# Stick-breaking scores of two heads in two 64-row halves of the PE array, with one transposition bank instead of two

## The chip, the cores and the metric

The kernel runs on one core of one Trainium2 chip. The metric is the device time of one execution in microseconds (us). PE is TensorE, the matrix engine; DVE, ACT and POOL are VectorE, ScalarE and GpSimd; SP issues DMAs.

## The reference

One layer: RMSNorm, one input projection, eight stick-breaking heads and four differential heads, a gate, one output projection with the residual, a final RMSNorm. 1024 tokens and 16 meta tokens, width 1024, all float32. The part that the change touches is the scores z and the weights w made of them:

```python
for t0 in range(0, Lp, Q_BLOCK):                       # Q_BLOCK = 128, head width d = 64
    z = einsum('bqhd,bkhd->bhqk', q[:, t0:t1], k[:, :t1]) * d ** -0.5
    strict = arange(t1)[None, :] < arange(t0, t1)[:, None]
    log_beta = log_sigmoid(z)
    log_keep = where(strict, log_sigmoid(-z), 0.0)
    stick = pad(cumsum(log_keep[..., 1:], axis=3, reverse=True), ...)
    w = where(strict, exp(log_beta + stick), 0.0)
    o = einsum('bhqk,bkhd->bqhd', w, v[:, :t1])
```

## The kernel before

Tokens run in reverse order, so that the stick-breaking product is a forward scan. The work is cut into eight groups: groups 0 to 3 hold two stick-breaking heads each, groups 4 to 7 one differential head each. A float32 product is made of float32r passes over an exact hi + lo split of both operands.

While a group's attention runs, the four projections of the next group (q, v, k, gate: `mm3`, L154 to L156, three passes per k-tile) are woven into it: `weave` takes from either generator by a ratio of planned times. A scheduler then sets the final order on each engine, and gives tiles the buffers that are free at that place of its plan. Each engine works through its own list in that order. So PE finds projection products between the steps of the attention, and where the list has none, it stands until the step before has come through the other engines.

One stick-breaking group goes over 8 query blocks of 128 rows; block b sees 1040 - 128 b keys. In what follows b0 is the widest (1040 columns, in chunks of 348, 346, 346), b1 has 912 (2 x 456), b2 784, b3 656, b4 528, b5 400, b6 272, b7 144. A step for one head and one block (a head-block):

- `qk` (L461, L462): scores. q is stacked as [hi; lo] in 128 rows, k hi and k lo are each there twice, so two passes of 128 rows carry the three products. Tiles z, three PSUM banks.
- `sb_weights`: the mask on the first 128 columns (DVE, L473), two sigmoids per chunk (ACT, L474 to `keep`, L475 to `beta`), the scan over `keep` (DVE, L478), its product with `beta` (DVE, L480), a small copy (POOL, L481). `beta` and `keep` come from a pool of four buffers with the tag be.
- `sb_transpose`: 128 x 128 transpositions of beta (PE, L499) in batches of up to four into a bank tr, each batch copied to wt by ACT (L500). Two tr banks.
- `sb_pv` (L521): weights times v for two blocks; the two heads stand in two 64-column halves of the array.

The heads take turns: transposition of head 0's last block, scores and weights of head 0, the same for head 1. `stack_q` and `stack_k` make the doubled operands with moves by DMA on SP's queue: nine in a stick-breaking group. Groups 4 to 7 use the same `qk` with their own stacking, and the same z and tr banks (transpositions at L624 and L658, copies at L625).

Of the kernel before, what the change touches and what calls it, by code (L numbers as in the profile page):

```python
"""Hybrid trunk layer: stick-breaking heads and differential heads side by side.

Tokens run in reverse order on the chip (r = 1039 - position): the stick-breaking
product is then a forward scan, and a query block sees a suffix of the keys.
float32 products run as three float32r passes over an exact hi + lo split of both
operands; where a head is only 64 deep, q is stacked [hi; lo] so that two passes
over the duplicated k hi and k lo carry the whole product.
"""
# [17 lines left out]
P = 128  # L26
D = 1024
SEQ = 1024
# [24 lines left out]
class Build:  # L53
# [15 lines left out]
    # ---------------------------------------------------------------- pools  # L69
    def open(self):  # L70
# [4 lines left out]
            for t, n in (("mm", 2), ("z", 3), ("tr", 2), ("pv", 1))  # L75
# [12 lines left out]
    # ------------------------------------------------------------ constants  # L88
# [21 lines left out]
    def df_constants(self):  # L110
# [8 lines left out]
        # -lambda on every partition  # L119
# [16 lines left out]
    # ----------------------------------------------------------- projection  # L136
    def w_half(self, u, h, copy=None, room=None):
        """load half of a 128-column unit of w_in and split it into hi + lo"""
# [8 lines left out]
    def mm3(self, ps, w, kt, c0, cn):  # L147
        """one k-tile of a projection, three passes"""
# [18 lines left out]
    def proj_last(self, u, chs, post):  # L167
        """the last projection goes k-tile by k-tile, and w_out takes the place of x behind it"""
# [30 lines left out]
    def evac_rope(self, t):  # L199
        """t = x * cos + swap(x) * sin, with rstd in both tables"""  # L200
# [14 lines left out]
    def stack_q(self, t, st, sb):  # L215
        """[hi; lo] for the first 64-deep half, [hi; lo] for the second, scale folded in"""
# [3 lines left out]
        lo = self.tl(self.tp, [P, T], F32R, "t")[:, :SEQ]  # L220
# [3 lines left out]
        if sb:  # L224
            self.move(b[0:64], a[64:128])
            self.move(b[64:128], lo[64:128])
            self.move(a[64:128], lo[0:64])
        else:
            for r in (0, 64):
                self.move(b[r + 32:r + 64], a[r + 32:r + 64])  # L230
                self.move(b[r:r + 32], lo[r + 32:r + 64])
                self.move(a[r + 32:r + 64], lo[r:r + 32])
        st["q"] = (a, b)

    def stack_k(self, t, st, sb):
        """[hi; hi] and [lo; lo] for both halves"""
        nc = self.nc
        ha, hb, la, lb = (self.tl(self.a2, [P, T], F32R, n) for n in ("ha", "hb", "la", "lb"))
        nc.scalar.copy(out=ha, in_=t)
        nc.vector.tensor_sub(la, t, ha.bitcast(F32))  # L240
        for a, b in ((ha, hb), (la, lb)):
            for r, n in ((0, 64),) if sb else ((0, 32), (64, 32)):
# [5 lines left out]
    def make_v(self, t, st, sb, on_pe):  # L248
        """token-major v tiles: by transposition on PE where they are needed soon, else by
        32x32 transposition on DVE, the blocks put in place by DMA"""  # L250
# [26 lines left out]
    def make_vr(self, st, sb):  # L277
        """the rows of v that the tiles leave out"""
# [16 lines left out]
    def make_gate(self, g, sb):  # L295
        """g * sigmoid(g); among exponentials the sigmoid waits for the whole width, to
        change the function table once"""
# [28 lines left out]
    def project(self, gi, st, first=False):  # L326
        """generator: the four projections of a group and what attention needs of them"""
# [34 lines left out]
    def start(self, st):  # L362
        """x arrives k-tile by k-tile: split it, collect its squares, and run q, k, g of group 0"""
        nc, i = self.nc, self.i
        uq, uk, uv, ug = self.units(0)
        # the array clock rises under load: bring it up while the first tiles travel
# [10 lines left out]
        plan = [(uq, CH_Q, "mm"), (uk, CH_K, "z"), (ug, CH_Q, "tr")]  # L377
        banks = [[self.bank(tag) for _ in chs] for _, chs, tag in plan]
# [86 lines left out]
    def sb_weights(self, st, hd, b):  # L465
# [4 lines left out]
        for c0, cn in chunks(kw):  # L470
            z = self.qk(st, hd, b, c0, cn)
            if c0 == 0:
                nc.vector.tensor_add(z[:, :P], z[:, :P], self.zmask)  # L473
# [451 lines left out]
```

## Time and profile before

| what | value |
|---|---|
| median of 3 runs | 703.42 us (702.63 to 705.86) |
| profiled execution, from its first to its last instruction | 703.8 us |
| PE busy | 683.9 us (97%) |
| DVE busy | 510.6 us (73%) |
| ACT busy | 367.2 us (52%) |

The profiled execution has no time of its own besides its span, which lies 0.4 us above the median of the runs. Busy time of PE is the union of its products as they are drawn; a product is drawn longer than the distance to the next one, since products overlap in the array. What one of them costs is therefore read from the distance between starts, not from its length.

### The profile page before, as it was taken

The page shows a single profiled execution, that of the slowest core. Times are in us where ns is not written, and L with a number is a line of the kernel's source. Part 1 is how long each engine was busy: PE and PEld are TensorE (multiplying, and loading weights), DVE is VectorE, ACT ScalarE, POOL GpSimd, SP SyncE. Part 2 cuts the span into 40 slices and gives each one's busy share as a digit, 9 for nine tenths or more (in the row PEclk, how much of TensorE's full clock was granted, in tenths as well). Part 3 has the DMA queues.
Part 4 walks back from the last instruction along what each step waited for, and adds up shares of the span by engine and source line. Part 5 has one row for each costly group of instructions (what it writes and reads, how often), then busy time and mean ns, then how long its engine had stood idle before and what let it go on. Part 6 is the DMA issues. An engine that isn't in the chain of part 4 may idle for free.

```text
span 703.8 us, 11492 instructions
## 1 busy us (share of the span) xinstructions
PE 683.9 (97%) x4016; PEld 590.8 (84%) x4016; DVE 510.6 (73%) x1028; ACT 367.2 (52%) x961; POOL 150.0 (21%) x195
## 2 busy tenths in 40 slices
PE   8899999999999999989999999999999999999996
PEld 6699988788978897778878998899889987888885
DVE  6945887589667975697856877787678688777653
ACT  6512655555545554655543656555655545665542
POOL 4711011212011211131220112211212053011222
PEclk9999999999999999999999999999999999999998
DMA  8317224122341225122351225132503663221322
GB/s 306 121 46 167 75 48 113 53 62 65 76 100 61 61 57 126 38 60 61 61 136 60 62 60 136 32 93 59 137 30 90 157 235 128 64 83 61 117 86 94
DMA packets 59049, 64.67 MB, mean 92 GB/s; under 512 B 31088, under 2 KB 39408, under 8 KB 58992
## 3 DMA queue, kind: packets, MB, share of 16 engines
q1 hardware_dynamic: 58848, 63.94, 32.8%
q8 instruction: 32, 0.52, 0.3%
q14 instruction: 25, 0.20, 0.1%
q10 hardware_dynamic: 144, 0.00, 0.0%
HBM read 34.37 MB, written 7.34 MB: 59 GB/s over the span
## 4 chain that ended last, share of the span: by engine, by line
PE 82%; DVE 10%; issue 2%; DMA 2%; ACT 2%; POOL 1%; SPq 0%; POOLq 0%; DVEq 0%; ACTq 0%
PE mm L154 15%; PE mm L155 15%; PE mm L156 14%; PE mm L703 10%; PE pv L521 6%; PE tr L499 4%; PE z L461 4%; PE z L462 4%; PE pv L641 4%; PE tr L624 2%; DVE be L478 1%; DVE nm L580 1%; DVE xl L393 1%; DVE wt L144 1%; DMA t<-xT 1%
## 5 line engine op out<-in xcount | busy, mean ns | idle before, releaser
L154 PE MATMUL mm<-xh,wh 128*128 128x346 f32 (+2 forms) x592 | 211.8, 359 | 2.5 <-DVE be L208 2.0
L155 PE MATMUL mm<-xl,wh 128*128 128x346 f32 (+2 forms) x592 | 210.8, 356 | 0.4 <-DVE xl L393 0.3
L156 PE MATMUL mm<-xh,wl 128*128 128x346 f32 (+2 forms) x592 | 211.0, 357 | 0.0
L154 PEld LDWEIGHTS mm<-xh,wh 128*128 128x128 f32 x592 | 112.4, 190 | 13.0 <-DVE be L208 2.7
L156 PEld LDWEIGHTS mm<-xh,wl 128*128 128x128 f32 x592 | 112.3, 190 | 10.7 <-issue 1.7
L155 PEld LDWEIGHTS mm<-xl,wh 128*128 128x128 f32 x592 | 112.5, 190 | 9.7 <-issue 1.5
L478 DVE TENSOR_TENSOR_SCAN be<-be,zero 128x1040 f32<-128x1040 f32 (+7 forms) x64 | 92.7, 1449 | 28.1 <-ACT be L474 28.0
L590 ACT ACTIVATE be<-z,nm 128x346 f32<-128x346 f32 (+8 forms) x112 | 59.9, 540 | 48.1 <-DVE nm L587 27.8
L474 ACT ACTIVATE be<-z 128x456 f32<-128x456 f32 (+8 forms) x112 | 50.2, 461 | 58.6 <-DVE z L473 29.3
L481 POOL COPY rem<-be 16x16 f32<-16x16 f32 x64 | 29.1, 455 | 205.7 <-DVE be L480 198.9
L500 ACT COPY wt<-tr 128x512 f32<-128x512 f32 (+3 forms) x96 | 44.5, 488 | 41.8 <-PE tr L499 36.5
L475 ACT ACTIVATE be<-z 128x346 f32<-128x346 f32 (+8 forms) x112 | 49.0, 463 | 20.4 <-DVE be L480 18.2
L580 DVE TENSOR_REDUCE nm<-z 128x1 f32<-128x346 f32 (+8 forms) x112 | 54.1, 501 | 6.0 <-PE z L462 5.2
L480 DVE TENSOR_TENSOR be<-be,be 128x1039 f32<-128x1039 f32 (+7 forms) x64 | 50.8, 794 | 6.6 <-ACT be L475 2.8
L143 ACT CAST wh<-wraw 128x512 fp32r<-128x512 f32 x58 | 36.3, 627 | 35.7 <-PE mm L155 26.7
L144 DVE TENSOR_TENSOR wl<-wraw,wh 128x512 fp32r<-128x512 f32 x61 | 43.4, 713 | 11.1 <-ACT wh L143 10.9
L649 POOL TENSOR_TENSOR rr<-rr,mhalf 128x1 f32<-128x1 f32 x32 | 20.0, 625 | 139.0 <-DVE rr L648 103.0
L499 PE MATMUL tr<-ident,be 128*128 128x128 f32 x288 | 44.9, 276 | 0.7 <-DVE be L480 0.7
L521 PE MATMUL pv<-wt,v 128*64 128x256 f32 (+1 forms) x336 | 45.6, 357 | 0.0
L499 PEld LDWEIGHTS tr<-ident,be 128*128 128x128 f32 x288 | 34.1, 140 | 10.4 <-issue 6.1
L461 PE MATMUL z<-ha,qa 128*128 128x346 f32 (+8 forms) x112 | 37.7, 340 | 1.7 <-ACT be L590 1.7
L461 PE MATMUL z<-hb,qb 128*128 128x346 f32 (+8 forms) x112 | 38.3, 342 | 0.5 <-ACT be L475 0.3
(215 smaller groups left out, 1252.3 us busy)
## 6 DMA issues: line engine op xcount, KB each, us to landing
wraw<-w_in SPq DMA_DIRECT2D x64, 256.0 KB, 2.7
t<-w_out SPq DMA_DIRECT2D x8, 512.0 KB, 3.8
t<-xT SPq DMA_DIRECT2D x7, 520.0 KB, 5.5
v<-t SPq DMA_DIRECT2D x96, 32.0 KB, 2.0
mix_scratch<-gate SPq DMA_DIRECT2D x6, 512.0 KB, 3.8
t<-mix_scratch SPq DMA_DIRECT2D x16, 192.0 KB, 2.4
hb<-ha SPq DMA_DIRECT2D x8, 260.0 KB, 3.7
lb<-la SPq DMA_DIRECT2D x8, 260.0 KB, 4.6
```

Of the source, the lines that this page charges most:

```text
L144: nc.vector.tensor_sub(lo, raw, hi.bitcast(F32))
L154: nc.tensor.matmul(o, hi[:, k, :], xh, start=kt == 0, stop=False)
L155: nc.tensor.matmul(o, hi[:, k, :], xl, start=False, stop=False)
L156: nc.tensor.matmul(o, lo[:, k, :], xh, start=False, stop=kt == KT - 1)
L461: nc.tensor.matmul(z[:, :cn], q, st["kh"][hd][:, s], start=True, stop=False)
L478: nc.vector.tensor_tensor_scan(out=keep[:, :kw], data0=keep[:, :kw], data1=self.zero.to_broadcast([P, kw]), initial=1.0, op0=ALU.mult, op1 ...
L480: nc.vector.tensor_mul(beta[:, 1:kw], beta[:, 1:kw], keep[:, :kw - 1])
L499: nc.tensor.transpose(tr[:, m * P:(m + 1) * P], w[:, c:c + P], self.ident)
L521: nc.tensor.matmul(pv[r, s], st["v"][:, b + j, r], w, start=p in ends[0], stop=p in ends[1])
L580: nc.vector.tensor_reduce(out=nm[:, comp, j:j + 1], in_=z[:, :cn], op=ALU.max, axis=AX.X, negate=True)
L590: nc.scalar.activation(p[:, c0:c0 + cn], zs[j][:, :cn], AF.Exp, bias=bias, accum_out=sm[:, comp, j:j + 1])
L703: self.nc.tensor.matmul(ps[:, :cn], a, b[kt][:, w], start=first and n == 0, stop=last and n == 2)
```

## The change

In the stick-breaking groups q and k are no longer stacked: q hi, q lo, k hi, k lo each hold head 0 in rows 0 to 63 and head 1 in rows 64 to 127. `qk_rows` makes both heads' scores of a chunk in two z banks, each head in its own 64 rows of the array, in three passes: hi hi, hi lo, lo hi. The nine moves of a group fall away. `sb_weights` handles both heads of a block and takes two beta and two keep tiles at once. Banks: four z, one tr. The order of a step is now: transposition of both heads' last block, then scores and weights of both. At the start, one of the two gate banks of group 0 is a z bank. Lines from L370 on move down by one, those behind `sb_weights` by 17.

```diff
-            for t, n in (("mm", 2), ("z", 3), ("tr", 2), ("pv", 1))
+            for t, n in (("mm", 2), ("z", 4), ("tr", 1), ("pv", 1))
...
     def stack_q(self, t, st, sb):
-        lo = self.tl(self.tp, [P, T], F32R, "t")[:, :SEQ]
+        lo = b if sb else self.tl(self.tp, [P, T], F32R, "t")[:, :SEQ]
...
-        if sb:
-            self.move(b[0:64], a[64:128])
-            self.move(b[64:128], lo[64:128])
-            self.move(a[64:128], lo[0:64])
-        else:
+        if not sb:
...
     def stack_k(self, t, st, sb):
+        if sb:
+            st["kh"], st["kl"] = ha, la
+            return
...
-        plan = [(uq, CH_Q, "mm"), (uk, CH_K, "z"), (ug, CH_Q, "tr")]
+        plan = [(uq, CH_Q, ("mm", "mm")), (uk, CH_K, ("z", "z", "z")), (ug, CH_Q, ("z", "tr"))]
...
+    def qk_rows(self, st, b, c0, cn):
+        z = [self.bank("z"), self.bank("z")]
+        (qh, ql), kh, kl = st["q"], st["kh"], st["kl"]
+        t = slice(b * P, (b + 1) * P)
+        s = slice(b * P + c0, b * P + c0 + cn)
+        for n, (q, k) in enumerate(((qh, kh), (qh, kl), (ql, kh))):
+            for hd in range(2):
+                r = slice(64 * hd, 64 * hd + 64)
+                nc.tensor.matmul(z[hd][:, :cn], q[r, t], k[r, s], start=n == 0, stop=n == 2)
+        return z
...
-    def sb_weights(self, st, hd, b):
+    def sb_weights(self, st, b):
...
-        beta = self.tl(self.a4, [P, T], F32, "be")
-        keep = self.tl(self.a4, [P, T], F32, "be")
+        beta = [self.tl(self.a4, [P, T], F32, "be") for _ in range(2)]
+        keep = [self.tl(self.a4, [P, T], F32, "be") for _ in range(2)]
         for c0, cn in chunks(kw):
-            z = self.qk(st, hd, b, c0, cn)
-            if c0 == 0:
-                nc.vector.tensor_add(z[:, :P], z[:, :P], self.zmask)
-            nc.scalar.activation(keep[:, c0:c0 + cn], z[:, :cn], AF.Sigmoid, scale=-1.0)
-            nc.scalar.activation(beta[:, c0:c0 + cn], z[:, :cn], AF.Sigmoid)
-            yield 2 * cn * MM_NS
+            zs = self.qk_rows(st, b, c0, cn)
+            for hd, z in enumerate(zs):
+                if c0 == 0:
+                    nc.vector.tensor_add(z[:, :P], z[:, :P], self.zmask)
+                nc.scalar.activation(keep[hd][:, c0:c0 + cn], z[:, :cn], AF.Sigmoid, scale=-1.0)
+                nc.scalar.activation(beta[hd][:, c0:c0 + cn], z[:, :cn], AF.Sigmoid)
+            yield 3 * cn * MM_NS
...
             for hd in range(2):
                 if s > 0:
                     yield from self.sb_transpose(st, hd, s - 1)
-                if s < NB:
-                    yield from self.sb_weights(st, hd, s)
+            if s < NB:
+                yield from self.sb_weights(st, s)
```

The scheduler makes a new order of all this. Two places in the third stick-breaking group (group 2) show it. The first is PE's list from the transpositions of b3 on. Before, it has the scores of one head for b5 (z, 400 columns) with projection products (mm) behind them, and each transposition batch (tr) or product with v (pv) has its next batch some projection products further on:

```order
L499 MATMUL tr_490_2653<-ident_101,be_467_2539 128x128 x4
L521 MATMUL pv_497_2695<-wt_456_2481,v_317_1769 64x256
L156 MATMUL mm_495_2671<-xh7_10_131,wl_482_2597 128x346
L461 MATMUL z_502_2727<-ha_355_1985,qa_279_1558 128x400
L462 MATMUL z_502_2727<-la_357_1987,qa_279_1558 128x400
L154 MATMUL mm_503_2734<-xh0_3_124,wh_478_2590 128x346
L155 MATMUL mm_503_2734<-xl0_11_132,wh_478_2590 128x346
L156 MATMUL mm_503_2734<-xh0_3_124,wl_479_2591 128x346
L154 MATMUL mm_503_2734<-xh1_4_125,wh_478_2590 128x346
L155 MATMUL mm_503_2734<-xl1_12_133,wh_478_2590 128x346
```

With the change the same place has the six score products of b5, both transposition batches of b3 and the scores of b6 (272 columns), z_496 being head 0 and z_497 head 1:

```order
L476 MATMUL z_496_2771<-ha_348_2009,qa_275_1583 128x400
L476 MATMUL z_496_2771<-la_349_2010,qa_275_1583 128x400
L476 MATMUL z_496_2771<-ha_348_2009,qb_276_1584 128x400
L476 MATMUL z_497_2772<-ha_348_2009,qa_275_1583 128x400
L476 MATMUL z_497_2772<-la_349_2010,qa_275_1583 128x400
L476 MATMUL z_497_2772<-ha_348_2009,qb_276_1584 128x400
L516 MATMUL tr_474_2641<-ident_101,be_452_2533 128x128 x4
L516 MATMUL tr_475_2647<-ident_101,be_452_2533 128x128
L538 MATMUL pv_487_2730<-wt_446_2508,v_310_1787 64x256
L516 MATMUL tr_476_2653<-ident_101,be_453_2534 128x128 x4
L476 MATMUL z_515_2856<-ha_348_2009,qa_275_1583 128x272
```

The projection products are gone from this place, and the three passes of one head stand together, ahead of the three of the other. The second place is ACT's list over b3 and b4 of the same group. Before (be_460 and be_468 are keep of b3's heads, be_487 keep of b4's head 0):

```order
L474 ACTIVATE be_460_2496<-z_461_2497 128x328
L474 ACTIVATE be_460_2496<-z_462_2503 128x328
L143 CAST wh_481_2596<-wraw_480_2594 128x512
L475 ACTIVATE be_459_2495<-z_461_2497 128x328
L475 ACTIVATE be_459_2495<-z_462_2503 128x328
L500 COPY wt_456_2481<-tr_457_2482 128x4x128
L500 COPY wt_456_2481<-tr_458_2491 128x2x128
L474 ACTIVATE be_468_2540<-z_469_2541 128x328
L475 ACTIVATE be_467_2539<-z_469_2541 128x328
```

With the change (be_455 is keep of b3's head 1, be_480 keep of b4's head 0; tr_447 to tr_451 are the transpositions of b2):

```order
L489 ACTIVATE be_455_2536<-z_457_2538 128x328
L489 ACTIVATE be_455_2536<-z_459_2555 128x328
L517 COPY wt_446_2508<-tr_447_2509 128x4x128
L517 COPY wt_446_2508<-tr_448_2518 128x2x128
L490 ACTIVATE be_453_2534<-z_457_2538 128x328
L490 ACTIVATE be_453_2534<-z_459_2555 128x328
L517 COPY wt_449_2522<-tr_450_2523 128x4x128
L489 ACTIVATE be_480_2664<-z_482_2666 128x264
L489 ACTIVATE be_480_2664<-z_484_2680 128x264
L517 COPY wt_449_2522<-tr_451_2529 128x2x128
```

What moved: the keep sigmoids of b4's head 0 now stand behind a copy of a transposition batch of head 1 of b2, and both heads' keep tiles of a block lie between copies of both heads' transpositions; no weight cast (L143) stands between.

## Rows read from the trace of the kernel before

**Rows 1.** The page's parts 1, 2 and 4: busy time, PE's slices and clock, chain.
```profile
PE 683.9 (97%) x4016; PEld 590.8 (84%) x4016; DVE 510.6 (73%) x1028; ACT 367.2 (52%) x961; POOL 150.0 (21%) x195
PE   8899999999999999989999999999999999999996
PE 82%; DVE 10%; issue 2%; DMA 2%; ACT 2%; POOL 1%; SPq 0%; POOLq 0%; DVEq 0%; ACTq 0%
```

**Rows 2.** Windows over three stick-breaking groups: stretch, length, each engine's busy time, granted clock.
```profile
97.00:171.00 74.00, 74.00 (x452) 62.10 (x450) 56.14 (x80) 40.31 (x98) 11.95 (x22) 1.00 0.30 76
171.00:242.60 71.60, 71.60 (x441) 59.96 (x442) 53.19 (x75) 38.83 (x94) 8.63 (x21) 1.00 0.29 75
242.60:320.60 78.00, 75.02 (x446) 62.56 (x445) 57.30 (x86) 41.68 (x95) 16.59 (x24) 0.98 0.27 68
```

**Rows 3.** Timeline of PE, scores in a row: start, length, what.
```profile
101.67 0.31 PE L461 MATMUL z<-hb,qb 128*128 128x328 f32 x1
101.82 0.31 PE L462 MATMUL z<-lb,qb 128*128 128x328 f32 x1
101.97 0.31 PE L461 MATMUL z<-hb,qb 128*128 128x328 f32 x1
```

**Rows 4.** The chain in order of time: transpositions, and products with v.
```profile
77.03 0.87 PE tr L499 x8
...
97.33 3.38 PE pv L521 x28
```

**Rows 5.** Timeline of PE around short runs in 64-column and 64-row halves.
```profile
144.95 0.39 PE L155 MATMUL mm<-xl,wh 128*128 128x512 f32 x1
145.18 0.40 PE L156 MATMUL mm<-xh,wl 128*128 128x512 f32 x1
145.41 0.39 PE L154 MATMUL mm<-xh,wh 128*128 128x512 f32 x1
145.73 0.43 PE L521 MATMUL pv<-wt,v 128*64 128x128 f32 x2
146.10 0.27 PE L531 MATMUL tr<-ident,rem 64*128 64x64 f32 x1
146.30 0.49 PE L155 MATMUL mm<-xl,wh 128*128 128x512 f32 x1
146.73 0.43 PE L521 MATMUL pv<-wt,v 128*64 128x128 f32 x2
147.09 0.50 PE L156 MATMUL mm<-xh,wl 128*128 128x512 f32 x1
```

**Rows 6.** Groups by line: count, busy and mean ns, idle before them and its releasers.
```profile
L478 DVE TENSOR_TENSOR_SCAN be<-be,zero 128x1040 f32<-128x1040 f32 (+7 forms) x64 | 92.7, 1449 | 28.1 <-ACT be L474 28.0
L480 DVE TENSOR_TENSOR be<-be,be 128x1039 f32<-128x1039 f32 (+7 forms) x64 | 50.8, 794 | 6.6 <-ACT be L475 2.8
L474 ACT ACTIVATE be<-z 128x456 f32<-128x456 f32 (+8 forms) x112 | 50.2, 461 | 58.6 <-DVE z L473 29.3 <-DVE be L480 16.1 <-PE z L462 11.3
L500 ACT COPY wt<-tr 128x512 f32<-128x512 f32 (+3 forms) x96 | 44.5, 488 | 41.8 <-PE tr L499 36.5 <-PE pv L521 5.0
L473 DVE TENSOR_TENSOR z<-z,zmask 128x128 f32<-128x128 f32 x64 | 18.4, 292 | 8.3 <-PE z L462 7.9
```

**Rows 7.** Timeline of DVE: one head-block's scan and product (784 columns).
```profile
98.45 1.76 DVE L478 TENSOR_TENSOR_SCAN be<-be,zero 128x784 f32<-128x784 f32 x1
100.32 0.97 DVE L480 TENSOR_TENSOR be<-be,be 128x783 f32<-128x783 f32 x1
```

**Rows 8.** Line L461: what ended PE's waits before it, us and times.
```profile
ACT be L590: 5.4, 9
ACT be L475: 0.8, 2
```

**Rows 9.** Windows before and after a wait of PE, columns as in rows 2.
```profile
308.00:313.50 5.50, 2.80 (x19) 2.17 (x18) 5.39 (x7) 1.49 (x4) 2.71 (x2) 1.00 0.15 48
313.60:317.00 3.40, 3.40 (x14) 3.40 (x13) 3.30 (x4) 2.37 (x5) 2.06 (x2) 0.50 0.01 2
```

More of the change, by code (lines that the diff above doesn't have):

```diff
@@ L237, in stack_k @@
         nc = self.nc
-        ha, hb, la, lb = (self.tl(self.a2, [P, T], F32R, n) for n in ("ha", "hb", "la", "lb"))
+        ha, la = (self.tl(self.a2, [P, T], F32R, n) for n in ("ha", "la"))
         nc.scalar.copy(out=ha, in_=t)
         nc.vector.tensor_sub(la, t, ha.bitcast(F32))
+        if sb:
+            st["kh"], st["kl"] = ha, la
+            return
+        hb, lb = (self.tl(self.a2, [P, T], F32R, n) for n in ("hb", "lb"))
         for a, b in ((ha, hb), (la, lb)):
-            for r, n in ((0, 64),) if sb else ((0, 32), (64, 32)):
+            for r, n in ((0, 32), (64, 32)):
                 self.move(b[r:r + n], a[r + n:r + 2 * n])
@@ L376, in start @@
         acc = self.tl(self.a4, [P, T], F32, "be")
-        plan = [(uq, CH_Q, "mm"), (uk, CH_K, "z"), (ug, CH_Q, "tr")]
-        banks = [[self.bank(tag) for _ in chs] for _, chs, tag in plan]
+        plan = [(uq, CH_Q, ("mm", "mm")), (uk, CH_K, ("z", "z", "z")), (ug, CH_Q, ("z", "tr"))]
+        banks = [[self.bank(tag) for tag in tags] for _, _, tags in plan]
         w = [[None, None] for _ in plan]
@@ L463, in qk @@
         return z
-    def sb_weights(self, st, hd, b):
+    def qk_rows(self, st, b, c0, cn):
+        nc = self.nc
+        z = [self.bank("z"), self.bank("z")]
[7 more added lines that the diff above has]
+        return z
@@ L477, in sb_weights @@
-        yield SB_PAD
-        nc.vector.tensor_tensor_scan(out=keep[:, :kw], data0=keep[:, :kw], data1=self.zero.to_broadcast([P, kw]),
-                                     initial=1.0, op0=ALU.mult, op1=ALU.add)
-        nc.vector.tensor_mul(beta[:, 1:kw], beta[:, 1:kw], keep[:, :kw - 1])
-        nc.gpsimd.tensor_copy(st["wrem"][32 * hd:32 * hd + 16, b], beta[:16, :16])
-        st["w", hd, b] = beta
+            zs = self.qk_rows(st, b, c0, cn)
[4 more added lines that the diff above has]
+                nc.scalar.activation(beta[hd][:, c0:c0 + cn], z[:, :cn], AF.Sigmoid)
@@ new lines, in sb_weights @@
+            yield 3 * cn * MM_NS
+        for hd in range(2):
+            yield SB_PAD
+            be, ke = beta[hd], keep[hd]
+            nc.vector.tensor_tensor_scan(out=ke[:, :kw], data0=ke[:, :kw], data1=self.zero.to_broadcast([P, kw]),
+                                         initial=1.0, op0=ALU.mult, op1=ALU.add)
+            nc.vector.tensor_mul(be[:, 1:kw], be[:, 1:kw], ke[:, :kw - 1])
+            nc.gpsimd.tensor_copy(st["wrem"][32 * hd:32 * hd + 16, b], be[:16, :16])
+            st["w", hd, b] = be
```

## The prediction

> **What bounds the kernel now.** I read the page first. PE is busy in 97% of the span and carries 82% of the chain; no slice is under eight tenths [rows 1]. Then the windows of three stick-breaking groups: PE is busy for 74.0 of 74.0, 71.6 of 71.6 and 75.0 of 78.0 us, while DVE has some 18 to 21 us free in each [rows 2]. So in these groups PE's list is the time: what lengthens it, and any hole in it, adds to the span; work saved on DVE, ACT or in DMAs is worth nothing as long as PE finds something else to do. The reader should see in rows 1 and 2 that there is no slack on PE to hide a cost in.
>
> What PE has in such a group is partly filler: the projections of the next group have no partner in the attention, and PE does them while a head-block goes through ACT and DVE. The second thing to look at is therefore how long that way is, and whether filler stands beside it in the new order.
>
> **The change, part by part.** *Columns streamed.* Scores start 0.15 us apart for 328 columns [rows 3], 0.457 ns a column. Before, four groups stream 4 groups x 2 heads x 2 passes x 4736 columns = 75,776, or 34.6 us. After, there are 336 products with 113,664 columns: 51.9 us one after another, 26.0 us if each has its partner of the other head beside it. Do halves of the array work side by side? For 64-column halves the trace says yes: a full transposition pass of 128 columns takes 0.87/8 = 0.109 us, a pass of the products with v, mostly 256 columns, 3.38/28 = 0.121 us [rows 4], half of what its columns would ask for; and those alternate between the heads. For 64-row halves no row shows it. I take it that they do too, as the nearest row does, but that each half works through its own products in the list's order. The list rarely alternates. It has 65 separate runs of score products; only 14 read 0,1,0,1,0,1 by head; 16 read 0,0,0,1,1,1, where only the third and fourth overlap, and 22 are the three passes of one head alone. Going through all 65 runs by that rule leaves 84,340 columns, 38.5 us. Cost: +3.9 us; ends -8.6 (all paired) and +17.3 (none).
>
> The Trainium skill, page "TensorE: Matmul & The Clock Gate", section "The mechanism" in its part on packing, says that products to different row groups run together, but start strictly in the list's order; by it the sum is the same +3.9, and a pairing that ignores the order is excluded. Its page "TensorEngine Tiling (Array Packing)", section "Theoretical Speedup", gives up to 2x for a contraction of at most 64; taken for all products that would be the -8.6. No run here shows either for row halves.
>
> *Changes of the array's form.* A run in halves costs at both ends. From 146.30 to 147.09 stand one 512-column product (0.23 apart from the next, as at 144.95 to 145.41) and two passes of 128 columns (0.109 each): 0.45 us of streaming in 0.79 us [rows 5]. So two changes cost 0.34 us, 0.17 each. For 64-row halves there is the transposition at 146.10: the next product starts 0.20 us later, at least 0.09 more than its columns ask for, and the product behind it starts 0.43 us on, again late [rows 5]. In PE's list I count 90 changes of form before (full, 64-column, 64-row) and 206 after: +116 x 0.17 = +19.7 us. Ends: 0.09 each, 10.4 us; 0.20 each, 23 us. On a PE without slack nothing hides this, except where PE would stand anyway (next part).
>
> *The way of a head-block.* Two keep and two beta tiles of one block now fill the four be buffers. In the built list, 41 of the 63 scans follow a scan whose keep tile lay in the same buffer (24 before), so the sigmoids cannot start before the product with beta has read it; and head 0's keep sigmoids wait on ACT behind a copy of head 1's transpositions, as the second place of the order shows. Nothing then runs beside DVE but filler, and the filler is badly spread: PE's list has five stretches of more than 30 rows without a projection product (32, 39, 33, 123 and 38 rows); before, the longest had 23. The longest goes from the products with v of b2 and b3 in the third group through b4 to b7 and into b0 of the fourth. It holds ten head-blocks' ways with 4384 of a group's 9472 columns (two heads). By the means of rows 6: scans and products with beta (92.7 + 50.8)/4 x 0.463 = 16.6 us; keep sigmoids 50.2/4 x 0.463 = 5.8; ten copies of 0.49, 4.9; ten masks of 0.29, 2.9; three hand-overs each of about 0.1 us, as the 0.11 us between a scan's end and its product [rows 7], 3.0. Sum 33.2 us. PE has in it 60 score products (7.1 us by the rule above), 46 transpositions (5.0), 29 products with v of two passes each (7.0) and 34 changes of form (5.8): 24.9 us. It stands for the rest, 8.3 us. The other four have 142 rows together; by the same share of rows, another 9.6. I take +18. Ends: 5, if sigmoids and copies overlap better than their list; 35, if DVE's other work of these groups (56.1 - 35.9 - 4.6 = 15.6 us in rows 2 and 6) stands in the way too.
>
> *One tr bank, four z banks.* Two transposition batches in a row now wait for the copy between them: 0.49 us [rows 6] and hand-overs, some 0.6. PE's list has 29 such pairs; 11 lie in the stretches above or near them and are counted there; 18 are in the differential groups and the last stage, +11 us. Ends: 0, if PE would have waited for something else there, and 20, as these groups lose filler in the same way (their lists too have long pieces without it now). A fourth z bank can give back at most PE's waits for a z bank, 6.2 us [rows 8], most of them behind exponentials; I take nothing, since the chain through DVE is what the bank would wait for.
>
> *Moves, masks, sigmoids.* The 36 moves that fall away are not on the chain (DMA 2% in rows 1, with PE full in rows 2): nothing. Sigmoids, masks, scans are as many as before: nothing.
>
> Sum: 703.8 + 3.9 + 19.7 + 18 + 11 = 756.4 us, against the profiled execution's span, which is 0.4 us above the median. I predict **756 us**.
>
> **Rivals.** *A. PE's work alone.* The filler suffices, since real lists are less serial than I count: 703.8 + 3.9 + 19.7 = 727 us. For it: DVE's free 20 us a group. Against it: the 123 rows.
>
> *B. The row halves run one after the other.* Then scores take 51.9 us, 13.4 more than in my sum; about a third of that falls where PE stands anyway: 765 us. For it: no row shows two row halves at once. Against it: the column halves do run together.
>
> *C. Faster.* Products of the other half are taken ahead of their place, over the change of form, so that all 336 are paired and a change costs nothing; the fourth z bank ends the waits of rows 8: 703.8 - 8.6 - 6.2 = 689 us. It decides only from a change of form under (8.6 + 6.2)/116 = 0.13 us, with no added idle; rows 5 have 0.17, and the 64-row transposition there shows no sign of being free.
>
> **How the numbers follow.** My sum 0.62, with a range of its own from 738 to 776; A 0.18; B 0.13; C 0.07. The range runs from A's 727, less a little, to the sum with the upper ends of two of its terms: 725 to 786. A measurement of this kernel tells about 0.5% from no change (3.5 us; the three runs before lie 3.2 us apart). Faster, half and more of C: 0.05; within 0.5%, the rest of C: 0.03; slower, all else: 0.92. One thing lies outside the terms: after a wait of PE near 312 us the granted clock fell from 1.00 to 0.50 for 3.4 us [rows 9], so from 2.4 to 1.2 GHz; with more and longer waits this will come more often. Part of the upper end is for that.
>
> **What would show it.** Columns: in an alternating run, scores of the two heads start in pairs, a few ns apart; in a run 0,0,0,1,1,1 only one pair does; single-file throughout means B. Changes of form: some 0.1 us more than streaming ahead of the first score of a run, and again at and behind its end; no such gap means C or A without its 19.7. The way of a head-block: PE's busy time under 95%, with idle ahead of transpositions, released by DVE's product with beta, in tens of us in total; DVE's wait ahead of its scan, 28.1 us in rows 6, near or above 50; the longest hole at the end of the third group, before the fourth group's b0. One tr bank: idle ahead of transpositions released by ACT's copy, or waits for it, in the differential groups. The prediction would be wrong if PE stays at 97% with these groups longer only by the changes of form (A), or if the groups take about as long as in rows 2.

## The result, and the profile after

| | before | after |
|---|---|---|
| median of 4 runs each | 703.80 us (702.63 to 705.86) | 837.61 us (836.44 to 838.61) |
| profiled span | 703.8 us | 835.0 us |
| PE busy | 683.9 us | 759.9 us |
| mean granted clock of PE | 0.992 | 0.939 |

The ratio is 1.189 (95% interval 1.186 to 1.193). The change is slower, as predicted, but by 134 us where 52 were predicted, and outside the range.

The page of the changed kernel, its parts 1, 2 and 4 as in [rows 1], with the slices of the granted clock:

```profile
PE 759.9 (91%) x4128; PEld 618.6 (74%) x4128; DVE 512.6 (61%) x1028; ACT 375.0 (45%) x961; POOL 138.5 (17%) x195
PE   8999999998999998779999997799888989688996
PEclk9999999998998987969999999899979999889999
PE 74%; DVE 9%; ACT 8%; issue 3%; DMA 3%; SPq 1%; POOL 0%; POOLq 0%; DVEq 0%; ACTq 0%
```

PE's even row of nines is gone. The holes come again from group to group, and the clock falls there. They don't stop at the stick-breaking groups: the second half of the row, whose code is the same but for the banks, has more of them.

What stands in the holes is seen if PE's products are taken in order and every piece of more than 6 us is marked in which no product of a projection (L154 to L156) or of the output (L703 before, L720 after) starts. Before there is none. After there are eight, 172.2 us in all. Windows over them, columns as in [rows 2]:

```profile
190.40:202.80 12.40, 8.78 (x49) 5.70 (x48) 12.23 (x20) 7.23 (x15) 4.18 (x6) 0.92 0.41 94
247.10:260.90 13.80, 11.55 (x70) 7.06 (x68) 9.85 (x20) 8.69 (x20) 1.75 (x5) 0.93 0.01 1
284.70:298.90 14.20, 10.56 (x53) 7.29 (x53) 12.63 (x19) 7.71 (x17) 2.91 (x7) 0.79 0.39 88
315.50:360.50 45.00, 35.71 (x198) 22.41 (x196) 28.17 (x49) 24.83 (x62) 5.42 (x16) 0.78 0.07 21
400.10:412.40 12.30, 10.47 (x66) 6.51 (x65) 8.70 (x15) 6.34 (x18) 1.49 (x4) 0.86 0.05 8
510.40:534.10 23.70, 14.40 (x71) 11.54 (x71) 14.48 (x42) 15.62 (x47) 4.11 (x6) 0.78 0.07 22
599.10:619.20 20.10, 13.95 (x63) 10.72 (x64) 10.44 (x33) 14.51 (x43) 4.43 (x6) 0.75 0.04 14
707.30:738.00 30.70, 21.95 (x118) 17.40 (x118) 15.85 (x61) 20.78 (x61) 5.61 (x6) 0.83 0.15 48
sum 172.20, PE 127.37 PEld 88.65 DVE 112.34 ACT 105.72 POOL 29.90; mean PE 15.92 PEld 11.08 DVE 14.04 ACT 13.21 POOL 3.74
```

No engine is full there: PE 74%, DVE 65%, ACT 61%. The attention goes from engine to engine with nothing beside it. 44.8 of the 75.0 us in which PE is not busy at all lie here (the lengths less PE's busy time: 20.6 in the first five pieces, which lie in the stick-breaking groups, 24.2 in the last three), and the mean clock is between 0.75 and 0.93.

Inside the longest one, the timeline of PE and ACT shows what a step consists of (the idle time of the engine and what ended it in brackets):

```profile
320.61 0.44 PE L516 MATMUL tr<-ident,be 128*128 128x128 f32 x2
...
321.08 0.37 ACT L517 COPY wt<-tr 128x256 f32<-128x256 f32 x1 [0.53 <-PE tr L516]
321.35 0.79 ACT L490 ACTIVATE be<-z 128x328 f32<-128x328 f32 x2
...
321.51 0.66 PE L516 MATMUL tr<-ident,be 128*128 128x128 f32 x4 [0.46 <-ACT wt L517]
...
322.25 0.59 ACT L517 COPY wt<-tr 128x512 f32<-128x512 f32 x1
...
322.89 0.44 PE L516 MATMUL tr<-ident,be 128*128 128x128 f32 x2
```

Transpose, copy, transpose: the next batch starts when the copy has left the one bank, and a copy may stand behind two sigmoids on ACT. I call this a turn; 0.90 and 1.38 us from batch to batch here. The groups of lines that answer to [rows 6]:

```profile
L495 DVE TENSOR_TENSOR_SCAN be<-be,zero 128x1040 f32<-128x1040 f32 (+7 forms) x64 | 91.1, 1427 | 45.5 <-ACT be L489 45.4
L516 PE MATMUL tr<-ident,be 128*128 128x128 f32 x288 | 54.9, 304 | 9.1 <-ACT wt L517 8.3 <-DVE vr L293 0.5
L517 ACT COPY wt<-tr 128x512 f32<-128x512 f32 (+3 forms) x96 | 46.2, 481 | 115.5 <-PE tr L516 115.3
L462 PE MATMUL z<-ha,qa 128*128 128x346 f32 (+8 forms) x56 | 20.8, 377 | 7.9 <-ACT be L607 7.9
```

The scan waits 45.5 us in place of 28.1, and ACT's idle time ahead of the copies, ended by the transpositions, is 115.3 in place of 36.5. Of the prediction's signs, PE's share under 95% is there (91%), and the scan's wait comes near its 50. Idle time of PE ahead of transpositions was to be ended by DVE's product with beta, in tens of us; it is 9.1 us ahead of L516, and ACT's copy ended 8.3 of it. PE stands nearly as long for a score bank behind exponentials (7.9 us ahead of this form of L462). A list of waits shows where an engine stood, not what made it stand there.

The scores ran in pairs, and in more of them than the prediction's rule gave. Timeline of PE, one run whose passes alternate between the heads:

```profile
87.44 0.60 PE L516 MATMUL tr<-ident,be 128*128 128x128 f32 x4
87.97 0.45 PE L476 MATMUL z<-ha,qa 64*128 64x392 f32 x2
88.25 0.35 PE L476 MATMUL z<-la,qa 64*128 64x392 f32 x2
88.43 0.35 PE L476 MATMUL z<-ha,qb 64*128 64x392 f32 x2
88.71 0.43 PE L155 MATMUL mm<-xl,wh 128*128 128x346 f32 x1
```

Two products of 392 columns, one of each head, take 0.18 us together (88.25 to 88.43); at the 0.457 ns a column of [rows 3], one alone takes 0.18. The row halves run side by side.

The list shown under "The change" has the scores of b5 in group 2 as three passes of one head and then three of the other, and by the prediction's rule only the third and the fourth of such a run overlap. In the trace they run in pairs too:

```profile
324.56 0.81 PE L476 MATMUL z<-ha,qa 64*128 64x400 f32 x2
325.06 0.64 PE L476 MATMUL z<-la,qa 64*128 64x400 f32 x2
325.39 0.64 PE L476 MATMUL z<-ha,qb 64*128 64x400 f32 x2
```

Two products with the same operands are the two heads', so this place ran 0,1,0,1,0,1. By the starts 33 of the 65 runs are of this kind, where the prediction counted 14 in the list; the 22 runs of one head alone are there as counted. Whether the array took the second head's products ahead of their place, or the program's order differs here from the list that is printed, the trace does not tell.

### The profile page after: what moved, and what is told of

Same layout as the page of the kernel before. It is cut to its first block, busy times and chain, and to the rows that moved or that the text cites. A ratio compares the mean times of both kernels' runs of the same rounds, so it can differ in the third digit from the quotient of the medians.

```text
span 835.0 us, 11611 instructions
## 1 busy us (share of the span) xinstructions
PE 759.9 (91%) x4128; PEld 618.6 (74%) x4128; DVE 512.6 (61%) x1028; ACT 375.0 (45%) x961; POOL 138.5 (17%) x195
## 4 chain that ended last, share of the span: by engine, by line
PE 74%; DVE 9%; ACT 8%; issue 3%; DMA 3%; SPq 1%; POOL 0%; POOLq 0%; DVEq 0%; ACTq 0%
PE mm L154 13%; PE mm L156 13%; PE mm L155 13%; PE mm L720 9%; PE pv L538 5%; PE tr L516 5%; PE z L476 4%; PE pv L658 3%; PE z L462 2%; ACT be L607 2%; PE tr L641 2%; DVE be L495 2%; PE z L463 2%; DVE be L497 1%; ACT wt L517 1%
## 5 line engine op out<-in xcount | busy, mean ns | idle before, releaser
L154 PE MATMUL mm<-xh,wh 128*128 128x346 f32 (+2 forms) x592 | 217.9, 369 | 4.8 <-DVE be L208 4.1
L155 PE MATMUL mm<-xl,wh 128*128 128x346 f32 (+2 forms) x592 | 215.1, 363 | 0.1
L156 PE MATMUL mm<-xh,wl 128*128 128x346 f32 (+2 forms) x592 | 214.9, 363 | 0.1
L154 PEld LDWEIGHTS mm<-xh,wh 128*128 128x128 f32 x592 | 115.6, 195 | 23.1 <-issue 6.2
L156 PEld LDWEIGHTS mm<-xh,wl 128*128 128x128 f32 x592 | 115.9, 196 | 12.9 <-issue 2.8
L155 PEld LDWEIGHTS mm<-xl,wh 128*128 128x128 f32 x592 | 116.0, 196 | 11.0 <-issue 1.4
L495 DVE TENSOR_TENSOR_SCAN be<-be,zero 128x1040 f32<-128x1040 f32 (+7 forms) x64 | 91.1, 1427 | 45.5 <-ACT be L489 45.4
L517 ACT COPY wt<-tr 128x512 f32<-128x512 f32 (+3 forms) x96 | 46.2, 481 | 115.5 <-PE tr L516 115.3
L498 POOL COPY rem<-be 16x16 f32<-16x16 f32 x64 | 20.3, 318 | 274.1 <-DVE be L497 261.4
L143 ACT CAST wh<-wraw 128x512 fp32r<-128x512 f32 x58 | 35.9, 622 | 65.2 <-PE mm L155 49.7
L516 PE MATMUL tr<-ident,be 128*128 128x128 f32 x288 | 54.9, 304 | 9.1 <-ACT wt L517 8.3
L516 PEld LDWEIGHTS tr<-ident,be 128*128 128x128 f32 x288 | 36.3, 150 | 27.5 <-ACT wt L517 15.5
L538 PE MATMUL pv<-wt,v 128*64 128x256 f32 (+1 forms) x336 | 50.1, 372 | 0.0
L658 PE MATMUL pv<-v,wt 128*128 128x128 f32 x288 | 44.5, 297 | 1.1 <-ACT on L667 1.1
L658 PEld LDWEIGHTS pv<-v,wt 128*128 128x128 f32 x288 | 40.7, 212 | 4.0 <-ACT on L667 2.3
```

Source lines behind the costliest of these rows:

```text
L154: nc.tensor.matmul(o, hi[:, k, :], xh, start=kt == 0, stop=False)
L155: nc.tensor.matmul(o, hi[:, k, :], xl, start=False, stop=False)
L156: nc.tensor.matmul(o, lo[:, k, :], xh, start=False, stop=kt == KT - 1)
L495: nc.vector.tensor_tensor_scan(out=ke[:, :kw], data0=ke[:, :kw], data1=self.zero.to_broadcast([P, kw]), initial=1.0, op0=ALU.mult, op1=ALU ...
L516: nc.tensor.transpose(tr[:, m * P:(m + 1) * P], w[:, c:c + P], self.ident)
L517: nc.scalar.copy(out=wt[:, m0 + e:m0 + e + mn, e, :], in_=tr[:, :mn * P].rearrange("p (m c) -> p m c", c=P))
```

## The experiments

The change has two parts that the prediction had priced apart: the scores, and the banks. The theories: **scores** (form changes and columns), **room** (both heads' four weight buffers), **banks** (the single transposition bank), and for the last, what it acts through. The "planner" of the expectations is the scheduler that sets each engine's list. Where no rounds are named, a time is of a single execution; repeats of one kernel lie within 0.6% of each other.

**Banks and scores apart.** The kernel before with nothing changed but its banks:

```diff
-            for t, n in (("mm", 2), ("z", 3), ("tr", 2), ("pv", 1))
+            for t, n in (("mm", 2), ("z", 4), ("tr", 1), ("pv", 1))
-        plan = [(uq, CH_Q, "mm"), (uk, CH_K, "z"), (ug, CH_Q, "tr")]
+        plan = [(uq, CH_Q, ("mm", "mm")), (uk, CH_K, ("z", "z", "z")), (ug, CH_Q, ("z", "tr"))]
```

> The kernel before with nothing changed but the PSUM banks: four for scores, one for transpositions (and the opening projections placed to fit). Theory 'banks' (most of the loss in the differential groups and the last stage, whose code is the same in both kernels, +54 us by the two traces, comes from the single transposition bank): 750 to 765 us. The prediction's own term for that bank (+11, 0 to 20): 704 to 724 us. Theory 'scores' (the stick-breaking scores make the whole difference, what follows is only late): 704 to 710 us.

Measured: 810.51 us, before 702.21 beside it. The banks alone cost 108 us, more than any theory had said.

The other half: the changed kernel with those lines put back.

> The changed kernel with the PSUM banks of before: three for scores, two for transpositions; the scores stay in pairs of 64-row halves. Theory 'banks': 775 to 790 us (the 54 us of the later stages come back). Theory 'room' (both heads of a block need all four weight buffers at once) and theory 'scores': the stick-breaking groups stay as they are or get worse, since a pair now waits for two of three banks: 820 to 860 us.

Measured: 737.65 us. All theories missed it: the change without its banks is 100 us faster than the change, not 55. Its page:

```profile
PE 716.5 (97%) x4128; PEld 591.0 (80%) x4128; DVE 505.5 (69%) x1028; ACT 368.9 (50%) x961; POOL 144.2 (20%) x195
PE   8899999999999999999999999999999999999995
PEclk9999999999999999999999999999999999999999
```

PE's row is full again and no piece over 6 us lacks filler. The same kernel again, timed in four executions:

> The changed kernel with the banks of before, timed: the scores' own cost. By the prediction's two terms with this list's counts: 157 changes of form more x 0.17 = 26.7, and the columns by the list's order (97,066 x 0.457 ns = 44.4, against 34.6) 9.7: 704 + 36 = 740 us, ratio 1.051; if form changes cost 0.09 each, 728 us, 1.034.

Measured: 738.20 us against 704.46, ratio 1.048 (1.046 to 1.051). So the scores, with their new order of steps, cost 34 us, and these are PE's own work: its busy time is 716.5 against 683.9 us.

**Scores by turns.** The order, banks and buffers of before, but each head's scores in three passes in its own 64 rows:

```diff
+        r = slice(64 * hd, 64 * hd + 64)
+        for n, (q, k) in enumerate(((qh, kh), (qh, kl), (ql, kh))):
+            nc.tensor.matmul(z[:, :cn], q[r, t], k[r, s], start=n == 0, stop=n == 2)
```

> The kernel before (its banks, its order of heads, its weight buffers), with each head's scores as three passes in its own 64 rows, the heads by turns and not as pairs, and without the moves that stacked hi and lo. Columns alone: 4736 key columns of a group's blocks x 2 heads x 4 groups x 1 more pass = 37,900 columns, +16 us at 0.42 ns. Theory 'form changes' (0.35 to 0.4 us for each way into the 64-row form and back, now for each head's own chunks, some 200 to 270 ways): 704 + 16 + 70 to 110 = 790 to 830 us. Theory 'room' (the loss of the stick-breaking groups comes from the four buffers and the pairs, not from the form): 750 to 780 us.

Measured: 754.20 us (before 702.21), as the theory "room" expected and not "form changes" at 0.35 to 0.4. But "room" is not shown by it: with 113,664 - 75,776 columns more (17.3 us at 0.457 ns) and 187 changes of form more (277 in PE's products as they ran, 90 before) at the prediction's 0.17, the sum is 49.1, measured 52.0. It is the price of a form change in the expectation that was too high.

**Room.** The changed kernel with keep tiles in buffers of their own, and the same with the old banks:

```diff
-        keep = [self.tl(self.a4, [P, T], F32, "be") for _ in range(2)]
+        keep = [self.tl(self.a2, [P, T], F32, n) for n in ("hb", "lb")]
```

> The changed kernel, but the two keep tiles of a block take two buffers each of the tiles that the stick-breaking groups no longer fill with moved keys, so that a block's scores need not wait for the transpositions of the block before. Theory 'room': the stick-breaking groups lose most of their 77 us again beyond the form changes (24 to 30 us): 775 to 800 us. Theories 'banks' and 'form changes': 825 to 840 us.

> The changed kernel with the banks of before (738 us) and the keep tiles in buffers of their own, as in the run with more room. Theory 'room' (the step of the prediction that cost +18): 715 to 728 us. Theory 'room costs nothing where there are two transposition banks': 733 to 742 us.

Measured: 841.37 and 734.49 us. More room gains nothing with one bank and 3.7 us with two, about as much as repeats of a kernel can differ. The theory falls.

**Which bank.** The kernel before with three score banks and one transposition bank, the eighth bank used only at the start:

```diff
-            for t, n in (("mm", 2), ("z", 3), ("tr", 2), ("pv", 1))
+            for t, n in (("mm", 2), ("z", 3), ("tr", 1), ("pv", 1), ("sp", 1))
```

> The kernel before with three score banks as it had and one transposition bank; the eighth bank is used only by the opening projections. Theory 'one transposition bank' (a batch of transpositions waits for the copy of the batch before it, and the holes lower the granted clock): 790 to 825 us, about the 810 us of the run with four score banks and one for transpositions. Theory 'fourth score bank' (the list is made anew round it): 704 to 730 us.

Measured: 810.22 us (before 704.34). It is the transposition bank; in this kernel, whose scores are not paired, the fourth score bank neither helps nor harms.

**The turn.** Half batches, meant to let the bank's halves take turns (changed kernel), and copies shared by two engines, meant to shorten the turn (kernel of the run before this):

```diff
+        if tag == "tr":
+            self.half = 256 - self.half
+            return self.trb[:, self.half:self.half + 256]
...
-        for m0 in range(0, n, 4):
-            mn = min(4, n - m0)
+        for m0 in range(0, n, 2):
+            mn = min(2, n - m0)
```

```diff
-            nc.scalar.copy(out=wt[:, m0 + e:m0 + e + mn, e, :],
-                           in_=tr[:, :mn * P].rearrange("p (m c) -> p m c", c=P))
+            for copy, f, g in ((nc.scalar.copy, 0, (mn + 1) // 2), (nc.vector.tensor_copy, (mn + 1) // 2, mn)):
+                if g > f:
+                    copy(out=wt[:, m0 + e + f:m0 + e + g, e, :],
+                         in_=tr[:, f * P:g * P].rearrange("p (m c) -> p m c", c=P))
```

> The changed kernel, its one transposition bank used as two halves by turns, each for a batch of at most two transpositions with a copy of its own (more and shorter copies). Theory 'one transposition bank': a batch can be written while the one before it is copied, 750 to 790 us. Theory 'the copies' time in ScalarE's queue', not the bank, sets the pace: 835 to 870 us, since there are some 100 copies more.

> The kernel before with three score banks and one transposition bank (810 us), the copy of each batch shared: one half by ScalarE, the other by VectorE. Theory 'length of a turn': the copy of four blocks falls from 0.49 to some 0.3 us; by the 0.7 us that each of the 96 added turns cost in the run with half batches (0.69 us for a copy of 0.37 with its waits), 144 batches of the attentions save up to 0.15 us each: 780 to 800 us. Theory 'queues': a half now also waits behind VectorE's scans (1.45 us each), so the turn gets longer: 812 to 850 us.

Measured: 906.24 and 874.48 us. Both went beyond the bad end, and in neither did the edit do what it was meant to. Timeline of the half batches:

```profile
345.03 0.39 ACT L523 COPY wt<-tr 128x256 f32<-128x256 f32 x1
...
345.47 0.33 PE L522 MATMUL tr<-ident,be 128*128 128x128 f32 x1 [0.57 <-ACT wt L523]
```

The next half batch starts 0.05 us after the copy of the other half ends: it still waits for the whole bank. So the run has 324 turns in place of 224 and nothing overlapped. Of the shared copies, the groups by line:

```profile
L502 ACT COPY wt<-tr 128x256 f32<-128x256 f32 (+1 forms) x96 | 32.4, 338 | 125.4 <-PE tr L499 124.8 <-PE z L462 0.4
L502 DVE COPY wt<-tr 128x256 f32<-128x256 f32 (+1 forms) x80 | 29.1, 364 | 42.3 <-ACT wt L502 42.1
```

DVE stood 42.1 us for ACT's copy: the halves are copied one after the other. The Trainium skill, page "PSUM — Partial Sum Buffer", section "PSUM bank collisions raise a hardware error", says that no two engines may be in the same 32 partitions of a bank at once, two readers included, and that programs have to order them. The traces show programs that do so, with those 42.1 us and the 0.05 us above; what would happen without that order no run here shows.

The two runs do show that longer or more turns go with a longer time. Taken from the first transposition of a batch to the end of its last copy, the bank is held 1.36 us a turn in the run with one transposition bank and 1.65 us with shared copies: 224 x 0.29 = 65 us more, and the time is 64 us longer. With half batches it is 324 x 1.08 = 350 us against 224 x 1.32 = 296 in the changed kernel: 54 us more, and the time is 69 us longer. That is near, but no price of a turn by itself: the lists of these runs differ too.

**The list.** The same two pairs of banks with lists that the scheduler makes without its model of times:

```diff
-TC_OPTS = {"schedule_with_timeline_sim": True}
+TC_OPTS = {"schedule_with_timeline_sim": False}
```

> The kernel before with the list of each engine left in the order in which the program is written (no reordering by the planner). A base for the next run: 704 to 760 us.

> The same unplanned list with the banks of the change (four for scores, one for transpositions). Theory 'one transposition bank': 80 to 120 us over the unplanned kernel with two transposition banks. Theory 'planner' (the lists that the planner makes for one transposition bank put batches back to back and run out of projections, and the bank by itself costs little): within 25 us of it.

> The changed kernel with the lists made in the program's order of priority, without the planner's model of times. Theory 'planner's list' (with one transposition bank the planner takes projection products ahead while a batch waits for its bank, and the end of each group stands without them): like the kernel before without the model and with the banks of the change, 770 us, plus the 33 us that the scores cost with the old banks: 785 to 815 us, so faster than with the model (838). Theory 'the bank sets the pace whatever the list': 835 us and more.

Measured: 767.81, 769.81 and 792.16 us. Without the model one bank costs 2 us in place of 108, no more than repeats differ, and the changed kernel is 45 us faster than with it. So a single transposition bank does not force 810 us: the same banks, with another list, run in 769.81, which puts at least 41 of the 108 us on the list. The rest is not separated, since the kernel with two banks already loses 63 us without the model, and its PE stands 65.7 us in which a wait for the bank can hide. The order in which the program is written is not kept to the letter either way, so these are not the same list with a bank fewer. In the second run PE's waits by line begin thus:

```profile
PE tr L499 <- ACT wt L500: 8.6, 9, 1.9
PE z L461 <- ACT be L590: 8.4, 8, 2.5
PE tr L284 <- POOL on L271: 6.4, 3, 2.1
PE tr L628 <- ACT wt L625: 3.4, 8, 0.8
```

PE does stand for copies here, 12 us in these rows, but other waits got shorter by as much: in all it stands 60.6 us. Its products come in finer portions: projection products form 291 separate runs in the order on PE (259 with two banks and no model), against 140 in the kernel with the same banks and the model, and 240 in the kernel before.

**Holding projections back.** The hi cast of each projection weight takes a bias of zero made from the latest head-block, so that projections can't go far ahead; with one transposition bank, and as a control with two:

```diff
+            nc.scalar.activation(hi, raw, AF.Identity, bias=self.turn)
...
+        self.nc.vector.tensor_scalar(out=zb, in0=t, scalar1=0.0, scalar2=0.0, op0=ALU.mult, op1=ALU.add)
+        self.turn = zb
```

> The kernel before with three score banks and one transposition bank, made with the planner's model, but the hi parts of the projections' weights are cast with a bias of zero that is made from the latest head-block's weights, so that projections can't run far ahead of the attention. PE's list then has 3 stretches of 30 or more products without a projection or output product (108 rows, all in the differential groups and the last stage) in place of 7 (378 rows). Theory 'projections run ahead': of the 106 us that the one bank costs, the share of the stretches that are gone comes back, 70 to 80%: 725 to 760 us. Theory 'one bank's turn-round itself': 800 to 820 us.

> The control of the run before this one: the same zero bias in the kernel before, with its two transposition banks. Both theories: 700 to 720 us; what it is above 704 is the price of holding back itself.

Measured: 817.74 and 744.64 us (before 704.96). The forecast of "projections run ahead" fails: in the executed order the eight long pieces without filler became eighteen short ones with nearly the same sum, 186.8 us in place of 177.9. But the theory is not decided, since the control, which both theories had near 704, lost 40 us, with five such pieces (60.5 us) of its own. Set against its control, one bank costs 73 us here and not 106.

**A shared second bank.** The changed kernel with four score banks, and transpositions and products with v on two banks by turns:

```diff
-            for t, n in (("mm", 2), ("z", 4), ("tr", 1), ("pv", 1))
+            for t, n in (("mm", 2), ("z", 4), ("tr", 2))
...
+        tag = "tr" if tag == "pv" else tag
```

> The changed kernel with four score banks, and two banks that transpositions and the products with v share by turns. PE's list has 3 stretches of 30 or more products without filler (124 rows) in place of 8 (396 rows). Theory 'projections run ahead': between the 738 us of the run with two banks of their own and the 838 us of the change, by the share of rows 738 + 100 x 124/396 = 770 us, 755 to 785. Theory 'any wait for a transposition bank': 800 us and more, since a product with v now holds one of the two.

Measured: 778.66 us, within the first theory's range; four pieces without filler, 73.2 us. Even a second bank that is shared with the products with v brings 59 us back.

**One relation over all of them.** The sum of the pieces over 6 us without a projection or output product, and what the kernel loses against the same scores with two transposition banks (the kernel before, measured beside it; 738.2 for the pairs; 734.5 for the pairs with more room):

| kernel | pieces, their sum | loss | loss per us |
|---|---|---|---|
| before; pairs with old banks, with more room too; by turns | none | 0 | |
| held back, two banks | 5, 60.5 us | 39.7 us | 0.66 |
| shared second bank | 4, 73.2 us | 40.5 us | 0.55 |
| change with more room | 9, 169.3 us | 106.9 us | 0.63 |
| the change | 8, 172.2 us | 99.4 us | 0.58 |
| before, three score banks, one for transpositions | 8, 177.9 us | 105.9 us | 0.60 |
| before, banks of the change | 8, 179.5 us | 108.3 us | 0.60 |
| held back, one bank | 18, 186.8 us | 112.8 us | 0.60 |
| copies shared | 11, 241.7 us | 170.0 us | 0.70 |
| half batches | 13, 278.6 us | 168.0 us | 0.60 |

With the scheduler's model, 0.55 to 0.70 us are lost for each us in which the attention has PE to itself. This is a relation between two measured sums; that the pieces are what costs is argued from it. The three kernels made without the model don't follow it: they have 12 to 20 us of such pieces, and the one with the old banks and scores already loses 63 us, with DVE on 23% of its chain in place of 10%.

## Why the prediction was wrong

**What bounds the kernel:** right. PE's list is the time, and a hole in it costs.

**Columns and changes of form** (+3.9 and +19.7): the price of a change is right, the count of columns is not. The prediction let only passes overlap that the list brings together; by their starts, passes were paired more often. If two products that start within half of a product's own time count as one, the changed kernel streams at most some 75,000 columns in place of the predicted 84,340, so no more than the 75,776 of before: 0 us in place of +3.9. With the old banks, where PE has 87 runs of scores and 55 of them are one head alone, the same count gives 89,352 columns, 6.2 us over [rows 3]'s price of the old 75,776 (the list's order, which the expectation used, gave 97,066 and 9.7). The measured 33.7 us leave 27.5 for 157 changes of form more, 0.175 each against 0.17. A run of three passes of one head shows that each end delays two products (timeline of PE, pairs with old banks):

```profile
97.14 0.32 PE L156 MATMUL mm<-xh,wl 128*128 128x346 f32 x1
97.39 0.41 PE L476 MATMUL z<-ha,qa 64*128 64x328 f32 x1
97.65 0.31 PE L476 MATMUL z<-la,qa 64*128 64x328 f32 x1
97.80 0.31 PE L476 MATMUL z<-ha,qb 64*128 64x328 f32 x1
98.04 0.43 PE L154 MATMUL mm<-xh,wh 128*128 128x346 f32 x1
98.30 0.33 PE L155 MATMUL mm<-xl,wh 128*128 128x346 f32 x1
98.46 0.32 PE L156 MATMUL mm<-xh,wl 128*128 128x346 f32 x1
```

Without a change of form the starts lie 0.15 to 0.16 us apart (97.65 to 97.80, 98.30 to 98.46); at the change 0.25 and 0.24, and behind it 0.26 both times: 0.4 us for two changes where nothing hides it. The Trainium skill, page "TensorEngine Tiling (Array Packing)", section "Key Properties", says that a change of tiling mode drains the array; the trace agrees, with 0.09 us ahead of the first product at each end. What its own 116 changes cost the changed kernel can't be read apart from its other losses.

**One transposition bank** (+11, ends 0 and 20): the step that failed. It read PE's list, found 18 back-to-back pairs of batches outside the long pieces and charged each 0.6 us. The waits it expected are there and about as large as it said: 15.5 us of PE's waits are for wt copies (8.3 ahead of L516, 7.2 ahead of the short transposition in the differential groups, by the waits of PE by line). But alone the bank costs 106 to 108 us, and on top of the scores 99. It goes with another list: made with one bank, the list has pieces that hold the attention alone, turn after turn, in both kinds of group, and the filler that PE would have had there stands elsewhere, in long runs. The list made without the model shows that at least 41 us of the cost are the list's and not the bank's; how the rest divides between the list and the turn is open. The term's reason for its upper end, that the differential groups lose filler too, named the loss and gave it 9 us more: in their three pieces PE stands 24.2 us, and the clock falls there too.

**The way of a head-block** (+18): the pieces were seen (32, 39, 33, 123 and 38 rows of PE's list), but given to the wrong part of the change. They were put down to the four weight buffers. More buffers give back nothing with one bank and 3.7 us with two; with the old banks the pieces are gone although the buffers are as few. The one list at hand held both changes, and nothing in it told which had made the pieces. Working out a list for each part alone would have told. The size came near by luck: PE was expected to stand for 18 us in five stretches of 265 rows, and in the five pieces of the stick-breaking groups it is idle for 20.6, though what made them was the bank and not the buffers.

**The clock, left outside the sum:** with the same products, PE is busy 43.5 us longer in the changed kernel than with the old banks (759.95 and 716.46). The mean granted clock is 0.939 against 0.998. Of the changed kernel's span, 101.6 us are at 0.50, so at 1.2 GHz, and PE is drawn busy in 84.3 of them; half of that, 42 us, is what the low level cost, nearly all of the 43.5. So the 99.3 us between the two spans are 55.8 in which PE stands more and 43.5 in which it is busy longer, by the clock in the main. Of the second, the prediction had the sign and no number.

**Moves, masks, sigmoids, the fourth score bank** (nothing): in the kernel before with one transposition bank, the fourth score bank costs nothing, 810.5 and 810.2 us with and without it; with paired scores it was not tried alone. Nor were the moves; the scores' 34 us are explained without them.

**The rivals.** A (727 us, PE's work alone) is near what the scores come to with two transposition banks: 738. B falls: a pair of passes takes the 0.18 us of one. C falls as a price, since the scores alone cost 34 us and a change of form is not free; but passes were paired beyond the list's order, as it had it. The right size was in no rival, since none gave the bank a higher price.

**Still open:** why the scheduler's model of times leads to such lists with one bank. Whether it takes projections too early is not decided: held back, the sum of the pieces stayed, but holding back had a price of its own. The list made for two banks was not tried with one.

No run beats the kernel before. The nearest with paired scores, with the old banks and room for the keeps, takes 734.5 us.

## What to carry to other kernels

Where a scheduler makes the order from the buffers, price a buffer that is taken away by the list it leads to, and not only by the waits for the buffer: make the lists for each part of a change alone, and look in them for pieces in which the bounding engine has nothing but the dependent chain. A bank that goes from one engine to another and back is held for the whole turn, queues included, and here a second one was worth 99 to 108 us, far more than the 15.5 us of waits for copies that PE showed without it. And where a hole is forecast on TensorE, the slower clock behind it belongs into the sum: here PE was busy 43.5 us longer, most of it by the clock, beside 55.8 us of added standing time.

## What the runs showed of the hardware

The granted clock fell to 0.50 while PE was far from idle. In the 6.9 us ahead of 323.8 us of the changed kernel, at 1.00, PE is drawn busy for 5.79 us and its longest hole, which ends at 324.18, is 0.84 us; from 323.8 on come 10.2 us at 0.50, in which it is drawn busy for 9.15. Windows of the changed kernel, columns as in [rows 2]:

```profile
316.90:323.80 6.90, 5.79 (x46) 3.50 (x42) 3.98 (x7) 3.97 (x11) 0.38 (x2) 1.00 0.10 38
323.80:334.00 10.20, 9.15 (x39) 5.74 (x41) 6.53 (x11) 5.35 (x15) 0.57 (x3) 0.50 0.01 2
```

A change of the array's form delays two products at each end, not one (0.09 and 0.11 us, then 0.09 and 0.10, beyond their streaming, in the run from 97.14 us above). And in these programs a PSUM bank was not used as two half banks: neither a transposition and a copy (0.05 us from the one's end to the other's start) nor two copies (42.1 us of waiting) were in it at the same time.
